# A two-layer encoder on one core: one more K pair per feed-forward block computed as seven products instead of eight, and silu as one activation function

## The chip, the core and the metric

The kernel runs on one core of one Trainium2 chip. A core has five engines that run side by side, each taking its own instructions in the order of the program: TensorE (PE in the profile; PEld is its loading of stationary operands), VectorE (DVE), ScalarE (ACT), GpSimd (POOL) and SyncE (SP, which here issues the DMAs). They wait for each other by semaphores. The metric is device time in microseconds (us) for one execution.

## The reference

The input is 256 tokens of 2048 float32. Layer 0 mixes tokens by differential attention and a gated spatial mixer, layer 1 by a bidirectional gated recurrence; each is followed by a feed-forward network. The change touches the feed-forward network (and one buffer count in layer 1's mixer):

```python
def swiglu(h, w_gate, w_up, w_down):
    return (jax.nn.silu(h @ w_gate) * (h @ w_up)) @ w_down

hn = rms_norm(h, ffn_norm[l])          # in both layers l = 0, 1
h = h + swiglu(hn, ffn_w_gate[l], ffn_w_up[l], ffn_w_down[l])
```

`w_gate` and `w_up` are 2048 x 5632, `w_down` is 5632 x 2048.

## The kernel before

Every matrix product is done in float32 accuracy from float32r operands: a weight tile `raw` arrives by DMA, ScalarE rounds it to `whi` (L310), VectorE computes the rest `wlo = raw - whi` (L320), and TensorE does three matmuls per product, `x_hi*w_hi`, `x_hi*w_lo`, `x_lo*w_hi` (L297 to L299).

**The feed-forward network.** The 5632 hidden columns are 11 blocks `j` of 512. They come in groups (0, 1), (2, 3, 4), (5, 6, 7), (8, 9, 10): for each block of a group `gate_up` computes gate and up for both halves (`b` = 0, 1) of the tokens; after a group the product with `w_down` of its blocks is added to `h` (`stream`, with lighter work for VectorE). The K dimension of 2048 is eight pairs `p` of two 128-row chunks. One DMA of 1 MB brings the four 128x512 weight blocks of a pair: gate and up, each for both chunks. Gate and up for both token halves of a pair are a 2x2 by 2x2 block product. `PAIRS` says how a pair is done in blocks 1 to 10 (block 0 is plain):

- `N`: eight products (24 matmuls) into four accumulators.
- `S`: seven products (21 matmuls) of sums of blocks, as in the Strassen-Winograd scheme, into seven accumulators `P1` to `P7`, which fill seven PSUM banks `ps0` to `ps6`. The sums of token blocks (`combos`) are made once per layer during block 0. The sums of weight blocks are made per pair: three additions on VectorE into `t` (L316, L317, L318), a cast to `thi` on ScalarE (L319) and `tlo = t - thi` on VectorE (L322). `whi` and `wlo` of such a pair have three parts and not four.

`t`, `thi` and `tlo` have one buffer each, `wlo` two, `raw` and `whi` three. The bank of an accumulator is free for the next block when VectorE or ScalarE has read it.

**The end of a block** (L425 to L450). After the last `S` pair, `u1`, `u2`, `u3` are formed from `P1`, `P6`, `P7` (L430 to L432). After the last pair VectorE forms `gs[0]` from `P2` and `gs[1]` from `P4` (L444, L445), `hh[0]` and `hh[1]` from `P5` (L446, L447), and adds `P3` to `hh[0]` (L448); silu follows as a sigmoid on ScalarE (L406) and a product on VectorE (L407); then `hh = hh * r * gs` (L410). In the next block `hh` is transposed on TensorE (L206, tiles `tp0`, `tp1`) into the operand of the `w_down` product.

**What sets the order.** The instructions of each engine are put in order when the program is built, by a planner with priorities: `high_priority(offset=AHEAD)` lets the weight preparation of a pair go ahead of other work, the block's end has twice that offset. TensorE's order is planned too: the first matmul of a product may stand ahead of products whose `wlo` or `tlo` comes later. On the chip each engine keeps the planned order.

Of the kernel before, what the change touches and what calls it, by code (L numbers as in the profile page):

```python
# [11 lines left out]
F32 = mybir.dt.float32  # L12
# [4 lines left out]
ALU = mybir.AluOpType  # L17
# [3 lines left out]
P = 128  # L21
# [51 lines left out]
def trunk(ctx: ExitStack, tc: tile.TileContext, ins, out):  # L73
# [210 lines left out]


    P1, P2, P3, P4, P5, P6, P7 = range(7)
    PAIRS = "NSNSNSNN"

    def gate_up(l, j, xs, combos, fx, name, plain, after):
        pattern = "N" * 8 if plain else PAIRS  # L290
        bk = [bank("mm", [P, NB], f"{name}_ps{i}") for i in range(4 if plain else 7)]
        uses = {"S": [P1, P2, P3, P6, P7, P4, P5], "N": [0, 1, 2, 3] if plain else [P2, P4, P5, P3]}
        seen, final = set(), {b: p for p in range(8) for b in uses[pattern[p]]}

        def product(b, p, x, w, end):
# [6 lines left out]
        for p in range(8):  # L302
# [28 lines left out]
            def w(i):  # L331
                return whi[:, i], wlo[:, i]

            if plain:
                for b, c, i in ((0, 0, 0), (0, 1, 1), (1, 0, 0), (1, 1, 1), (2, 0, 3), (2, 1, 2), (3, 0, 3), (3, 1, 2)):
                    product(b, p, x(c, b % 2), w(i), c == 1)
                    if (b, c) == (1, 1):
                        tick()
            elif fast:
                def sums(i):  # L340
                    return combos[p][0][:, i], combos[p][1][:, i]

                def tw(i):
                    return thi[:, i], tlo[:, i]

                product(P1, p, x(0, 0), w(0), True)
                product(P2, p, x(1, 0), w(1), True)
                product(P3, p, sums(2), w(2), True)
                product(P6, p, sums(1), tw(2), True)
                product(P7, p, sums(3), tw(1), True)  # L350
                product(P4, p, x(1, 1), tw(3), True)
                product(P5, p, sums(0), tw(0), True)
            else:
                for c in range(2):
                    product(P2, p, x(c, 0), w(c), c == 1)
                for c in range(2):
                    product(P4, p, x(c, 1), w(c), c == 1)
                for c in range(2):
                    product(P5, p, x(c, 1), w(3 - c), c == 1)
                for c in range(2):  # L360
                    product(P3, p, (combos[p][0][:, c], combos[p][1][:, c]), w(3 - c), c == 1)
# [4 lines left out]
    def make_combos(xs, cp, combos, name):  # L366

        for p in range(8):
            xh, xl = xs.get(p)
            xt = _ap(xh, 0, [[KG * S, 2], [S, KG], [1, S]]).bitcast(F32)  # L370
            k0 = p % 2 * 2
            n = 4 if PAIRS[p] == "S" else 2
            c = [cp.tile([P, n, P], F32R, tag=f"c{p}{i}", name=f"{name}_c{p}{i}", bufs=1) for i in range(2)]
            parts = tmp.tile([P, 2, n, P], F32, tag="hh", name=f"{name}_cp{p}", bufs=2)

            def x(k, b):
                return xt[:, :, k0 + k, b * P:(b + 1) * P]

            if n == 4:

                nc.vector.tensor_tensor(parts[:, :, 0], x(0, 1), x(1, 1), op=ALU.subtract)
                nc.vector.tensor_tensor(parts[:, :, 1], parts[:, :, 0], x(0, 0), op=ALU.subtract)
                nc.vector.tensor_tensor(parts[:, :, 2], parts[:, :, 1], x(1, 0), op=ALU.add)
                nc.vector.tensor_tensor(parts[:, :, 3], x(0, 0), x(0, 1), op=ALU.subtract)
            else:
                for k in range(2):
                    nc.vector.tensor_tensor(parts[:, :, k], x(k, 0), x(k, 1), op=ALU.subtract)
            nc.vector.tensor_tensor(parts[:, 0], parts[:, 0], parts[:, 1], op=ALU.add)
            nc.scalar.copy(c[0], parts[:, 0])
            nc.vector.tensor_tensor(c[1], parts[:, 0], c[0].bitcast(F32), op=ALU.subtract)  # L390
            combos.append(c)
            yield

    def ffn(l, xs, rstd, following):

        with tc.tile_pool(name=f"hT{l}", bufs=3, reuse_waits="tile") as hp:
# [5 lines left out]
                return rstd()[:, b:b + 1]  # L402

            def silu(g, src, b, n):
                sg = fx.tile([P, NB], F32, tag="u", name=f"{n}_s{b}", bufs=3)
                nc.scalar.activation(sg, src, AF.Sigmoid, scale=r(b))  # L406
                nc.vector.scalar_tensor_tensor(out=g, in0=src, scalar=r(b), in1=sg, op0=ALU.mult, op1=ALU.mult)  # L407

            def gated(out, src, b, g):
                nc.vector.scalar_tensor_tensor(out=out, in0=src, scalar=r(b), in1=g, op0=ALU.mult, op1=ALU.mult)  # L410
# [1 line left out]
            for blocks in (range(0, 2), range(2, 5), range(5, 8), range(8, 11)):  # L412
                halves = Lazy()
                for j in blocks:
# [18 lines left out]
                                early["u"] = u1, u2, u3  # L433

                    bk = gate_up(l, j, xs, combos, fx, n, plain, after)
                    hh = tmp.tile([P, 2, NB], F32, tag="hh", name=f"{n}_hh", bufs=2)
                    with tc.high_priority(offset=2 * AHEAD):
                        if plain:
                            for b in range(2):
# [425 lines left out]

    for nb in range(4):
        ps = proj_c(16 + nb, f"g{nb}", after=at_end(early) if nb == 3 else None)
        gt = tmp.tile([P, 2, NB], F32, tag="hh", name=f"g{nb}t", bufs=2)
        gated(ps, gt, True)
        if nb == 3:  # L870
            finish_pieces()
        nc.vector.tensor_tensor(o[nb], gt, o[nb], op=ALU.mult)
        xo.makers.append(lambda nb=nb: to_T(o[nb], xpool, "xT", f"co{nb}", gain_cols(SM_GN, nb)))
# [138 lines left out]
```

## Time and profile before

| | |
|---|---|
| time, three runs | 2432.55 to 2434.47 us, median 2433.96 us |
| the profiled execution | 2432.7 us, its span 2430.9 us |
| TensorE busy | 2403.7 us (99%), 11212 matmuls, mean granted clock 0.998 |
| VectorE busy | 1747.8 us (72%) |
| ScalarE busy | 1136.2 us (47%) |
| DMA | 445.50 MB, the weights' queue 52.1% of the 16 engines' span |

The span is from the first instruction to the last; the 1.8 us beside it lie around the span. A matmul is shown with a modelled duration that overlaps the next one, so its pace is read from starts, not from durations. A wait is shown as idle time before an instruction with the one that ended it.

### The profile page before, as it was taken

How to read it: one execution, taken by the hardware profiler on the slowest of the kernel's cores; microseconds unless marked ns; L12 is line 12 of the kernel's file. 1: busy time of each engine (PE TensorE's matmuls, PEld its weight loads, DVE VectorE, ACT ScalarE, POOL GpSimd, SP SyncE). 2: the span in 40 equal slices, each digit the busy share in tenths (PEclk: the TensorE clock that was granted, in tenths of full speed). 3: DMA queues.
4: the chain of work that ended last, by engine and by line, in shares of the span. 5: the costliest groups of instructions: out<-in, count | busy, mean ns of one | idle time of the engine just before them, and what ended most of it. 6: DMA issues, size and time to landing. Idle time of an engine off the chain costs nothing.

```text
span 2430.9 us, 27555 instructions
## 1 busy us (share of the span) xinstructions
PE 2403.7 (99%) x11212; PEld 1993.8 (82%) x11212; DVE 1747.8 (72%) x1680; ACT 1136.2 (47%) x1048; POOL 72.9 (3%) x72
## 2 busy tenths in 40 slices
PE   8999999999999999999999999999999999999998
PEld 7887878888888888888888888888788888888887
DVE  5658667688678678754758595855777867876884
ACT  5445454445345445454444444444444544544553
POOL 0003000000000000000000000000000000000002
PEclk9999999999999999999999999999999999999999
DMA  7444455555555555555444444445455555565553
GB/s 275 169 160 168 160 180 184 190 194 204 191 202 196 191 198 190 201 198 191 156 145 151 156 139 156 144 168 190 169 195 200 187 201 191 190 208 190 208 208 139
DMA packets 63135, 445.50 MB, mean 183 GB/s; under 512 B 6944, under 2 KB 7200, under 8 KB 9760
## 3 DMA queue, kind: packets, MB, share of 16 engines
q1 hardware_dynamic: 62576, 442.13, 52.1%
q8 instruction: 88, 1.44, 0.2%
q10 hardware_dynamic: 432, 1.60, 0.2%
q14 instruction: 39, 0.32, 0.0%
HBM read 441.61 MB, written 2.10 MB: 183 GB/s over the span
## 4 chain that ended last, share of the span: by engine, by line
PE 94%; DVE 3%; POOL 1%; issue 1%; DMA 1%; ACT 0%; SPq 0%; ACTq 0%; POOLq 0%; DVEq 0%
PE f_ps L298 12%; PE f_ps L297 12%; PE f_ps L299 12%; PE f0d_ps L164 3%; PE f0d_ps L166 3%; PE f0d_ps L165 3%; PE f1d_ps L164 3%; PE f1d_ps L165 3%; PE f1d_ps L166 3%; PE c_f_ps L166 2%; PE c_f_ps L164 2%; PE c_f_ps L165 2%; PE s_l L759 2%; PE c_q_ps L166 1%; PE c_q_ps L164 1%; PE c_q_ps L165 1%
## 5 line engine op out<-in xcount | busy, mean ns | idle before, releaser
L310 ACT CAST f_whi<-f_raw 128x2048 fp32r<-128x2048 f32 (+1 forms) x176 | 311.2, 1768 | 248.7 <-PE f_ps L299 162.5
L320 DVE TENSOR_TENSOR f_wlo<-f_raw,f_whi 128x2048 fp32r<-128x2048 f32 (+1 forms) x176 | 368.7, 2106 | 47.0 <-PE f_ps L298 33.2
L297 PE MATMUL f_ps<-f_whi,f_x 128*128 128x512 f32 x848 | 331.3, 393 | 6.1 <-DVE h L883 3.1
L299 PE MATMUL f_ps<-f_whi,f_x 128*128 128x512 f32 x848 | 330.3, 390 | 0.0
L298 PE MATMUL f_ps<-f_wlo,f_x 128*128 128x512 f32 x848 | 330.1, 389 | 0.0
L297 PEld LDWEIGHTS f_ps<-f_whi,f_x 128*128 128x128 f32 x848 | 159.2, 188 | 38.8 <-ACT f_j L182 6.9
L299 PEld LDWEIGHTS f_ps<-f_whi,f_x 128*128 128x128 f32 x848 | 159.2, 188 | 33.6
L298 PEld LDWEIGHTS f_ps<-f_wlo,f_x 128*128 128x128 f32 x848 | 159.3, 188 | 32.2
L322 DVE TENSOR_TENSOR f_tlo<-f_t,f_thi 128x2048 fp32r<-128x2048 f32 x60 | 137.3, 2288 | 62.7 <-ACT f_thi L319 62.7
L319 ACT CAST f_thi<-f_t 128x2048 fp32r<-128x2048 f32 x60 | 114.8, 1913 | 132.3 <-DVE f_t L318 120.0
L149 ACT CAST f1d__whi<-f1d__raw 128x2048 fp32r<-128x2048 f32 x44 | 84.4, 1919 | 128.4 <-PE f1d_ps L166 97.6
L150 DVE TENSOR_TENSOR f1d__wlo<-f1d__raw,f1d__whi 128x2048 fp32r<-128x2048 f32 x44 | 100.8, 2290 | 60.6 <-PE f1d_ps L165 33.0
L150 DVE TENSOR_TENSOR f0d__wlo<-f0d__raw,f0d__whi 128x2048 fp32r<-128x2048 f32 x44 | 100.7, 2289 | 59.0 <-PE f0d_ps L165 29.3
L149 ACT CAST f0d__whi<-f0d__raw 128x2048 fp32r<-128x2048 f32 x44 | 84.4, 1918 | 122.1 <-PE f0d_ps L166 91.3
L150 DVE TENSOR_TENSOR c_f_wlo<-c_f_raw,c_f_whi 128x2048 fp32r<-128x2048 f32 x32 | 73.3, 2292 | 72.5 <-PE c_f_ps L165 60.5
L164 PE MATMUL c_f_ps<-c_f_whi,c_x 128*128 128x512 f32 x256 | 102.5, 400 | 0.0
L299 PE MATMUL f_ps<-f_whi,x_c 128*128 128x512 f32 x260 | 101.1, 389 | 0.0
L298 PE MATMUL f_ps<-f_wlo,x_c 128*128 128x512 f32 x260 | 101.1, 389 | 0.0
L297 PE MATMUL f_ps<-f_whi,x_c 128*128 128x512 f32 x260 | 101.1, 389 | 0.0
L166 PE MATMUL c_f_ps<-c_f_whi,c_x 128*128 128x512 f32 x256 | 100.2, 392 | 0.0
L165 PE MATMUL c_f_ps<-c_f_wlo,c_x 128*128 128x512 f32 x256 | 99.6, 389 | 0.0
L149 ACT CAST c_f_whi<-c_f_raw 128x2048 fp32r<-128x2048 f32 x32 | 61.2, 1913 | 77.6 <-PE c_f_ps L166 57.6
(536 smaller groups left out, 5637.1 us busy)
## 6 DMA issues: line engine op xcount, KB each, us to landing
f_raw<-in_w_gu SPq DMA_DIRECT2D x176, 1024.0 KB, 4.9
f0d__raw<-in_w_down SPq DMA_DIRECT2D x44, 1024.0 KB, 4.9
f1d__raw<-in_w_down SPq DMA_DIRECT2D x44, 1024.0 KB, 4.9
c_f_raw<-in_hgrn_w_in SPq DMA_DIRECT2D x32, 1024.0 KB, 4.9
eout_raw<-in_even_w_out SPq DMA_DIRECT2D x16, 1024.0 KB, 4.8
c_i_raw<-in_hgrn_w_in SPq DMA_DIRECT2D x16, 1024.0 KB, 4.8
c_q_raw<-in_hgrn_w_in SPq DMA_DIRECT2D x16, 1024.0 KB, 4.8
c_g_raw<-in_hgrn_w_in SPq DMA_DIRECT2D x16, 1024.0 KB, 4.9
```

What stands on the lines that cost most here:

```text
L149: nc.scalar.copy(whi[:, d], raw[:, d])
L150: nc.vector.tensor_tensor(wlo[:, d], raw[:, d], whi[:, d].bitcast(F32), op=ALU.subtract)
L164: nc.tensor.matmul(ps[b], xh[:, k, sl], hi[:, k, :], start=first, stop=False)
L165: nc.tensor.matmul(ps[b], xh[:, k, sl], lo[:, k, :], start=False, stop=False)
L166: nc.tensor.matmul(ps[b], xl[:, k, sl], hi[:, k, :], start=False, stop=end)
L297: nc.tensor.matmul(bk[b], xh, hi, start=b not in seen, stop=False)
L298: nc.tensor.matmul(bk[b], xh, lo, start=False, stop=False)
L299: nc.tensor.matmul(bk[b], xl, hi, start=False, stop=end and final[b] == p)
L310: nc.scalar.copy(whi[:, d], raw[:, d])
L319: nc.scalar.copy(thi, t)
L320: nc.vector.tensor_tensor(wlo[:, d], raw[:, d], whi[:, d].bitcast(F32), op=ALU.subtract)
L322: nc.vector.tensor_tensor(tlo, t, thi.bitcast(F32), op=ALU.subtract)
```

## The change

Four things change. (1) `PAIRS` goes from `NSNSNSNN` to `SNSNSNSN`: four of eight pairs are `S`, from the first pair of a block on, and the last pair is `N`. `combos` follow. (2) In an `S` pair the product `P3` is issued fifth and not third. (3) silu is one activation function on ScalarE, in place; the sigmoid's tile and the VectorE product (L407) go. (4) Tiles with the tag `hh` (a block's `hh`, the parts of `combos`, and `gt` in layer 1's mixer) have one buffer and not two.

```diff
--- before.py
+++ after.py
@@ -284,12 +284,12 @@
 
 
     P1, P2, P3, P4, P5, P6, P7 = range(7)
-    PAIRS = "NSNSNSNN"
+    PAIRS = "SNSNSNSN"
 
     def gate_up(l, j, xs, combos, fx, name, plain, after):
         pattern = "N" * 8 if plain else PAIRS
         bk = [bank("mm", [P, NB], f"{name}_ps{i}") for i in range(4 if plain else 7)]
-        uses = {"S": [P1, P2, P3, P6, P7, P4, P5], "N": [0, 1, 2, 3] if plain else [P2, P4, P5, P3]}
+        uses = {"S": [P1, P2, P6, P7, P3, P4, P5], "N": [0, 1, 2, 3] if plain else [P2, P4, P5, P3]}
         seen, final = set(), {b: p for p in range(8) for b in uses[pattern[p]]}
 
         def product(b, p, x, w, end):
@@ -345,9 +345,9 @@
 
                 product(P1, p, x(0, 0), w(0), True)
                 product(P2, p, x(1, 0), w(1), True)
-                product(P3, p, sums(2), w(2), True)
                 product(P6, p, sums(1), tw(2), True)
                 product(P7, p, sums(3), tw(1), True)
+                product(P3, p, sums(2), w(2), True)
                 product(P4, p, x(1, 1), tw(3), True)
                 product(P5, p, sums(0), tw(0), True)
             else:
@@ -371,7 +371,7 @@
             k0 = p % 2 * 2
             n = 4 if PAIRS[p] == "S" else 2
             c = [cp.tile([P, n, P], F32R, tag=f"c{p}{i}", name=f"{name}_c{p}{i}", bufs=1) for i in range(2)]
-            parts = tmp.tile([P, 2, n, P], F32, tag="hh", name=f"{name}_cp{p}", bufs=2)
+            parts = tmp.tile([P, 2, n, P], F32, tag="hh", name=f"{name}_cp{p}", bufs=1)
 
             def x(k, b):
                 return xt[:, :, k0 + k, b * P:(b + 1) * P]
@@ -402,9 +402,7 @@
                 return rstd()[:, b:b + 1]
 
             def silu(g, src, b, n):
-                sg = fx.tile([P, NB], F32, tag="u", name=f"{n}_s{b}", bufs=3)
-                nc.scalar.activation(sg, src, AF.Sigmoid, scale=r(b))
-                nc.vector.scalar_tensor_tensor(out=g, in0=src, scalar=r(b), in1=sg, op0=ALU.mult, op1=ALU.mult)
+                nc.scalar.activation(g, src, AF.Silu, scale=r(b))
 
             def gated(out, src, b, g):
                 nc.vector.scalar_tensor_tensor(out=out, in0=src, scalar=r(b), in1=g, op0=ALU.mult, op1=ALU.mult)
@@ -433,7 +431,7 @@
                                 early["u"] = u1, u2, u3
 
                     bk = gate_up(l, j, xs, combos, fx, n, plain, after)
-                    hh = tmp.tile([P, 2, NB], F32, tag="hh", name=f"{n}_hh", bufs=2)
+                    hh = tmp.tile([P, 2, NB], F32, tag="hh", name=f"{n}_hh", bufs=1)
                     with tc.high_priority(offset=2 * AHEAD):
                         if plain:
                             for b in range(2):
@@ -865,7 +863,7 @@
 
     for nb in range(4):
         ps = proj_c(16 + nb, f"g{nb}", after=at_end(early) if nb == 3 else None)
-        gt = tmp.tile([P, 2, NB], F32, tag="hh", name=f"g{nb}t", bufs=2)
+        gt = tmp.tile([P, 2, NB], F32, tag="hh", name=f"g{nb}t", bufs=1)
         gated(ps, gt, True)
         if nb == 3:
             finish_pieces()
```

The planner puts the work in another order. Two places show it, both where block 4 of layer 0 follows block 3 within a group. `f0_4_` names a tile of layer 0, block 4; the digit after `wlo`, `whi`, `t`, `thi`, `tlo` is the pair; `ps0` to `ps6` are `P1` to `P7`; what stands in brackets is whom the instruction waits for.

TensorE before, at the seam of pair 0 (`N`, whose 24 matmuls open the block) and pair 1 (`S`), the first pair with a tile that VectorE makes after the end of block 3:

```order
L299 MATMUL f0_4_ps2_4299<-f0_4_whi0_4305,x0_c01_2813 128x512
L297 MATMUL f0_4_ps0_4297<-f0_4_whi1_4335,f00_x_2612 128x512 [waits DVE_49,Activation_49]
L297 MATMUL f0_4_ps1_4298<-f0_4_whi1_4335,f00_x_2612 128x512
L298 MATMUL f0_4_ps0_4297<-f0_4_wlo1_4336,f00_x_2612 128x512 [waits DVE_49]
L299 MATMUL f0_4_ps0_4297<-f0_4_whi1_4335,f00_x_2612 128x512
L298 MATMUL f0_4_ps1_4298<-f0_4_wlo1_4336,f00_x_2612 128x512
L299 MATMUL f0_4_ps1_4298<-f0_4_whi1_4335,f00_x_2612 128x512
```

TensorE now, from the eighth matmul of the block on (seven on pairs 0 and 1, on `whi0`, `wlo0` and `whi1`, stand ahead of it):

```order
L297 MATMUL f0_4_ps0_4298<-f0_4_whi2_4379,f01_x_2665 128x512 [waits Activation_49]
L206 MATMUL f0_3T_tp0_4371<-ident_89,f0_3_hh_4286 128x128 [waits DVE_49,PE_49]
L206 MATMUL f0_3T_tp0_4371<-ident_89,f0_3_hh_4286 128x128 x3
L298 MATMUL f0_4_ps1_4299<-f0_4_wlo1_4342,f00_x_2612 128x512 [waits DVE_49]
L299 MATMUL f0_4_ps1_4299<-f0_4_whi1_4341,f00_x_2612 128x512
L297 MATMUL f0_4_ps1_4299<-f0_4_whi1_4341,f00_x_2612 128x512
L298 MATMUL f0_4_ps1_4299<-f0_4_wlo1_4342,f00_x_2612 128x512
L299 MATMUL f0_4_ps1_4299<-f0_4_whi1_4341,f00_x_2612 128x512
L297 MATMUL f0_4_ps1_4299<-f0_4_whi2_4379,f01_x_2665 128x512
L206 MATMUL f0_3T_tp1_4443<-ident_89,f0_3_hh_4286 128x128 [waits DVE_49]
L206 MATMUL f0_3T_tp1_4443<-ident_89,f0_3_hh_4286 128x128 x3
L297 MATMUL f0_4_ps5_4303<-f0_4_thi0_4311,x0_c00_2812 128x512 [waits Activation_49]
```

The first matmul on `wlo1` stood behind 26 matmuls of block 4 and the transposes of block 3's `hh` behind 37; both stand behind 8 now, and the products of pair 0 on `thi0` behind them.

VectorE before, from the addition of `P3` of block 3 on:

```order
L448 TENSOR_TENSOR f0_3_hh_4281<-f0_3_ps2_4000,f0_3_hh_4281 128x512 [waits DVE_49,PE_49]
L407 SCALAR_TENSOR_TENSOR f0_3_g1_3997<-f0_3_g1_3997,f0_rstd_3003,f0_3_s1_4290 128x512 [waits Activation_49]
L410 SCALAR_TENSOR_TENSOR f0_3_hh_4281<-f0_3_hh_4281,f0_rstd_3003,f0_3_g0_3996 128x512 [waits DVE_49]
L410 SCALAR_TENSOR_TENSOR f0_3_hh_4281<-f0_3_hh_4281,f0_rstd_3003,f0_3_g1_3997 128x512 [waits DVE_49]
L318 TENSOR_TENSOR f0_4_t1_4339<-f0_4_t1_4339,f0_4_raw1_4334 128x512
L320 TENSOR_TENSOR f0_4_wlo1_4336<-f0_4_raw1_4334,f0_4_whi1_4335 128x1536
L320 TENSOR_TENSOR f0_4_wlo2_4379<-f0_4_raw2_4377,f0_4_whi2_4378 128x2048 [waits DMAHW6_49,PE_49,Activation_49]
L322 TENSOR_TENSOR f0_4_tlo1_4341<-f0_4_t1_4339,f0_4_thi1_4340 128x2048 [waits Activation_49]
L320 TENSOR_TENSOR f0_4_wlo3_4409<-f0_4_raw3_4407,f0_4_whi3_4408 128x1536 [waits DVE_49,DMAHW7_49,PE_49,Activation_49]
```

VectorE now, from the same addition on:

```order
L446 TENSOR_TENSOR f0_3_hh_4286<-f0_3_ps2_4000,f0_3_hh_4286 128x512 [waits DVE_49,PE_49]
L408 SCALAR_TENSOR_TENSOR f0_3_hh_4286<-f0_3_hh_4286,f0_rstd_3005,f0_3_g1_3997 128x512 [waits DVE_49,Activation_49]
L408 SCALAR_TENSOR_TENSOR f0_3_hh_4286<-f0_3_hh_4286,f0_rstd_3005,f0_3_g0_3996 128x512 [waits DVE_49]
L317 TENSOR_TENSOR f0_4_t0_4310<-f0_4_t0_4310,f0_4_raw0_4305 128x512
L320 TENSOR_TENSOR f0_4_wlo1_4342<-f0_4_raw1_4340,f0_4_whi1_4341 128x2048 [waits DMAHW5_49]
L318 TENSOR_TENSOR f0_4_t0_4310<-f0_4_t0_4310,f0_4_raw0_4305 128x512 [waits DVE_49]
L210 TENSOR_TENSOR f0_3T_x_4370<-f0_3T_tp0_4371,f0_3T_x_4370 128x512 [waits Activation_49]
L322 TENSOR_TENSOR f0_4_tlo0_4312<-f0_4_t0_4310,f0_4_thi0_4311 128x2048 [waits Activation_49]
L320 TENSOR_TENSOR f0_4_wlo2_4380<-f0_4_raw2_4378,f0_4_whi2_4379 128x1536 [waits DMAHW6_49,PE_49]
```

One instruction of silu is gone from between; the end of block 3 still stands ahead of the sums and the `wlo` of block 4's `S` pair, which is now pair 0 and not pair 1; `wlo1` is now the full tile of an `N` pair.

## Rows read from the trace of the kernel before

**Rows 1.** The page's busy times: engine, us, share of the span, instructions.
```profile
PE 2403.7 (99%) x11212; PEld 1993.8 (82%) x11212; DVE 1747.8 (72%) x1680; ACT 1136.2 (47%) x1048; POOL 72.9 (3%) x72
```

**Rows 2.** The page's chain that ended last, by engine.
```profile
PE 94%; DVE 3%; POOL 1%; issue 1%; DMA 1%; ACT 0%; SPq 0%; ACTq 0%; POOLq 0%; DVEq 0%
```

**Rows 3.** Windows of blocks 2, 3, 4 of layer 0, columns as named.
```profile
core 0: us, PE busy (x) PEld busy (x) DVE busy (x) ACT busy (x) POOL busy (x), PEclk, DMA share, GB/s
494.32:535.80 41.48, 41.48 (x184) 34.35 (x183) 33.59 (x26) 20.67 (x13) 0.00 (x0) 1.00 0.56 202
535.80:578.25 42.45, 42.45 (x193) 35.13 (x192) 36.57 (x34) 21.14 (x16) 0.00 (x0) 1.00 0.56 197
578.25:621.16 42.91, 42.91 (x193) 34.95 (x191) 37.19 (x33) 23.15 (x17) 0.00 (x0) 1.00 0.57 199
```

**Rows 4.** Timeline of PE, first matmuls of blocks 2 and 3: start, us.
```profile
494.32 0.39 PE L297 MATMUL f_ps<-f_whi,f_x 128*128 128x512 f32 x1
...
535.80 0.39 PE L297 MATMUL f_ps<-f_whi,f_x 128*128 128x512 f32 x1
```

**Rows 5.** Timeline of DVE, the end of block 3 and after: start, us.
```profile
578.98 0.68 DVE L448 TENSOR_TENSOR f_hh<-f_ps,f_hh 128x512 f32<-128x512 f32 x1
579.58 0.74 DVE L407 SCALAR_TENSOR_TENSOR f_g<-f_g,f_rstd,f_s 128x512 f32<-128x512 f32 x1
580.24 1.41 DVE L410 SCALAR_TENSOR_TENSOR f_hh<-f_hh,f_rstd,f_g 128x512 f32<-128x512 f32 x2
581.56 0.69 DVE L318 TENSOR_TENSOR f_t<-f_t,f_raw 128x512 f32<-128x512 f32 x1
582.16 1.76 DVE L320 TENSOR_TENSOR f_wlo<-f_raw,f_whi 128x1536 fp32r<-128x1536 f32 x1
...
588.24 1.76 DVE L320 TENSOR_TENSOR f_wlo<-f_raw,f_whi 128x1536 fp32r<-128x1536 f32 x1
589.90 1.22 DVE L316 TENSOR_TENSOR f_t<-f_raw 128x1024 f32<-128x1024 f32 x1
591.04 0.69 DVE L210 TENSOR_TENSOR f_3T_x<-f_3T_tp,f_3T_x 128x512 fp32r<-128x512 f32 x1
...
594.49 2.29 DVE L320 TENSOR_TENSOR f_wlo<-f_raw,f_whi 128x2048 fp32r<-128x2048 f32 x1 [1.44 <-PE f_ps L298]
596.70 2.29 DVE L322 TENSOR_TENSOR f_tlo<-f_t,f_thi 128x2048 fp32r<-128x2048 f32 x1
```

**Rows 6.** Timeline of PE, a matmul that completes a bank.
```profile
648.40 0.39 PE L166 MATMUL f0d_ps<-f0d__whi,f_4T_x 128*128 128x512 f32 x1
```

**Rows 7.** Timeline of DVE, the instruction that waited for it.
```profile
648.83 0.69 DVE L279 TENSOR_TENSOR h<-f0d_ps,h 128x512 f32<-128x512 f32 x1 [2.63 <-PE f0d_ps L166]
```

**Rows 8.** Timeline of DVE, a tlo that TensorE waited for.
```profile
789.69 2.28 DVE L322 TENSOR_TENSOR f_tlo<-f_t,f_thi 128x2048 fp32r<-128x2048 f32 x1
```

**Rows 9.** Timeline of PE, the matmul that waited for it.
```profile
792.03 0.50 PE L298 MATMUL f_ps<-f_tlo,x_c 128*128 128x512 f32 x1
```

**Rows 10.** Chain in order of time, eight transposes: start, us.
```profile
340.84 0.87 PE f_tp L206 x8
```

**Rows 11.** Groups of ACT and DVE instructions: count, busy us, mean ns, idle before.
```profile
L319 ACT CAST f_thi<-f_t 128x2048 fp32r<-128x2048 f32 x60 | 114.8, 1913 | 132.3 <-DVE f_t L318 120.0 <-PE f_ps L298 5.8 <-PE f_ps L299 5.0
L406 ACT ACTIVATE f_s<-f_g,f_rstd 128x512 f32<-128x512 f32 x40 | 28.9, 722 | 28.6 <-DVE f_g L444 15.4 <-DVE f_g L407 13.2
L406 ACT ACT_TABLE_LOAD x1 | 1.3, 1283 | 0.0
L407 DVE SCALAR_TENSOR_TENSOR f_g<-f_g,f_rstd,f_s 128x512 f32<-128x512 f32 x40 | 29.8, 747 | 1.5 <-ACT f_s L406 1.3
```

**Rows 12.** Timeline of PE, a wait as layer 0's feed-forward network begins.
```profile
362.84 0.47 PE L297 MATMUL f_ps<-f_whi,f_x 128*128 128x512 f32 x1 [3.00 <-DVE h L279]
```

**Rows 13.** Window around that wait, columns as in Rows 3.
```profile
360.00:365.00 5.00, 2.16 (x10) 1.83 (x11) 4.76 (x9) 4.10 (x7) 0.35 (x1) 1.00 0.37 110
```

## The prediction

> **What bounds the kernel now.** I read the page's busy times first: TensorE is busy 99% of the span, VectorE 72% [rows 1]. The chain that ended last says the same from the other side: 94% of it runs over TensorE and 3% over VectorE [rows 2]. So the time is the number of matmuls times their pace, as long as TensorE isn't kept waiting. The third view is windows over the stage that the change touches, three blocks of one group: 41.48, 42.45 and 42.91 us [rows 3]. Block 2 has 3 x 21 + 5 x 24 = 183 matmuls and nothing else on TensorE, and its first matmul stands 41.48 us ahead of block 3's [rows 4]: 41.48 / 183 = 0.2267 us a matmul. Blocks 3 and 4 hold eight transposes besides, 0.87 us [rows 10]; what is left over, 0.10 and 0.56 us, is waiting. The reader is to see two things in those windows: TensorE has no slack there, and VectorE rises from 33.6 to 36.6 to 37.2 us of about 42 [rows 3]. It is the second tightest engine, just where the change gives it more.
>
> **What goes.** One more S pair in each of the 10 fast blocks of two layers: 20 x 3 = 60 matmuls, 60 x 0.2267 = 13.6 us, all on the path, since TensorE is it. That is the whole gain. The product of silu on VectorE also goes, 40 x 0.747 us [rows 11], but off the path, except where the end of a block is.
>
> **What is added off the path.** An S pair costs VectorE three sums (1.22, 0.69, 0.69) and a tlo (2.29), less 0.53 for the smaller wlo (2.29 to 1.76) [rows 5]: 4.4 us a block, against 1.5 saved on silu. Block 4 would come to about 37.2 + 2.9 = 40.1 us. Its work on TensorE is 180 matmuls and eight transposes, 40.8 + 0.9 = 41.7 us, so VectorE still fits, with 4% to spare: as a sum it does not become the bound, but there is nothing left to make good a delay in the same block. ScalarE gets one thi more a block, 1.91 us [rows 11], and is busy 23 of 43 us [rows 3]. Silu stands where the sigmoid stood; I take its 0.72 us [rows 11]. Its table must be loaded in each layer, with the mixer's sigmoid table between: two more loads of 1.283 us [rows 11], on an engine that idles 20 us a block, taken as nothing (2.6 us if all of it showed). The single `hh` buffer costs nothing: a block's `hh` is read by transposes early in the next block and written again at that block's end.
>
> **What moves: the seam between blocks.** Before, a block began with an N pair, and its 24 matmuls, 5.4 us, covered the end of the block ahead. Now it begins with the S pair. Let T be the start of the new block's first matmul, and take block 3 to block 4 as the order gives it.
>
> VectorE's side. Its steps follow each other at 0.60 us for a 512-column addition (578.98 to 579.58), 0.66 for a product with two scalars, 1.14 for the first sum, 1.66 for a wlo of an S pair, 2.21 for a full wlo or a tlo [rows 5]. The last wlo of block 3 (pair 7) waits until TensorE has read the buffer for the last time in pair 5, 47 matmuls ahead of T: -10.65 us, and 0.43 from a matmul's start until a waiting VectorE starts (648.40 to 648.83) [rows 6, 7], so it starts at -10.2. From there VectorE has no gap: wlo, tlo of pair 6, wlo of the new pair 0, u2, gs[0], u3, first sum, gs[1], two hh: 2.21 + 2.21 + 1.66 + 3 x 0.60 + 1.14 + 3 x 0.60 = 10.8. The addition of P3, which needs the very last matmul (ready at +0.20), starts at +0.6. Then 0.60, the two products with gs (0.66 each, the last one lasting 0.75): hh is done at +2.6. A sum (0.60), and wlo1 from +3.1 to +5.4. The last sum ends at +6.0, and thi0 on ScalarE, 1.91 us, at +8.0.
>
> TensorE's side. Eight matmuls bring it to +1.8. It wants hh for four transposes and gets it at +2.7 (a wlo or tlo reaches a waiting matmul 0.06 us after its end, 791.97 to 792.03 [rows 8, 9]): 0.9 us of waiting. At +3.1 it wants wlo1, and gets it at +5.5: 2.4 us. Six matmuls and four transposes later, at +7.3, it wants thi0 and gets it at +8.0: 0.7 us. Then 11 matmuls end at +10.5, when tlo0 (8.0 + 2.3) is there. In all 3.9 us, in program order, with matmuls that could run standing behind. Behind wlo1 on VectorE stand the sum that thi0 needs and tlo0, so its delay is passed on.
>
> The first seam of a group (block 2 to 3) is different: coming from the light w_down stage, VectorE has made t0, thi0 and tlo0 before the end of block 2, and the same reckoning gives no wait. The order has the late form in blocks 4, 7 and 10 of both layers, word for word alike: six seams. Within a block the order puts first matmuls ahead of a late tlo, and the reckoning has each tlo there 0.0 to 0.3 us in time; I allow 0.05 us for each of the 48 S pairs of the later blocks of groups, 2.4 us.
>
> **The sum,** against the profiled execution's own 2432.7 us (span 2430.9): -13.6 for matmuls; +6 x 3.9 = +23.4 at the seams; -6 x 0.56 = -3.4, since the waiting that such a block has now is part of what is laid out anew; +2.4. That makes +8.8: 2441.5. The median of the runs is 1.3 above the profiled one, so 2443 us, slower by 0.4%.
>
> The seam is the term that the trace does not show, so both ends: below, VectorE not behind at T (0.4 less) and thi0 hidden (0.7 less), 2.8 us a seam, and the sum is 2436; above, tlo late by 0.3 us in each of those 48 pairs as well, 14.4 in place of 2.4, 2455. I take the reckoned 3.9, since every duration in it has a row and the order fixes who waits for whom.
>
> **Rivals.**
> - *Gain without the wait* (faster): TensorE finds something else to do, and 13.6 us come off whole: 2420. For: the blocks wait only 0.10 and 0.56 us now [rows 3], so the planner has hidden such things so far. Against: it hid them behind the N pair, and the order shows eight matmuls there. Chance 0.10.
> - *Short seam* (no change): the chain on VectorE is 0.4 us early and thi0 comes in time, no small waits: 6 x 2.8 - 3.4 - 13.6 = -0.2, 2434. Chance 0.14.
> - *VectorE becomes the bound all along a group*: 40.1 of 41.7 us leaves no room for its own waits, and each tlo of the 48 pairs comes 0.5 us late. The place is the tlo that TensorE waits for, and it decides from the point where VectorE's sum and waits pass 41.7 us: 2443 - 2.4 + 24 = 2465. For: in block 4 it idles 5.7 us, partly waiting for TensorE and thi [rows 3, 11]. Against: those waits shrink when it is late. Chance 0.09.
> - *The clock falls at the seams.* Rows: TensorE waited 3.00 us once, and the granted clock of that window was 1.00, the 2.4 GHz level [rows 12, 13]; the new waits are 2.4 us at most. If the clock halved after each seam for an S pair's 21 matmuls, 6 x 21 x 0.2267 = 28.6 us would be added: 2472. Chance 0.02. The Trainium skill, "TensorE: Matmul & The Clock Gate", section "HAM oscillation — how this bites in real kernels", speaks for this one: waits between groups of matmuls can put the clock back again and again. By that rule the time would be the 2472; the row of the 3.00 us wait doesn't bear it out.
>
> **How the numbers follow.** The forecast has 0.65. A difference under 0.2%, 4.9 us, can't be told from no change here, so slower is above 2438.8 and faster below 2429.1. Of the forecast's 0.65 about 0.04 lies under 2438.8 (a seam near its low end). Slower: 0.61 + 0.09 + 0.02 = 0.72; same: 0.14 + 0.04 = 0.18; faster: 0.10. The forecast's own range is 2436 to 2455. The range for 8 in 10 takes in the short seam and reaches a little towards the late tlo: 2432 to 2458.
>
> **What would show it.** Right: TensorE at 60 matmuls fewer; blocks 2, 5 and 8 at 40.8 us; block 3 near 41.7; blocks 4, 7 and 10 at 45 to 46, with waits ahead of a transpose, the first matmul on wlo1 and the first on thi0, put down to VectorE and ScalarE; VectorE without a gap from the last wlo to the new wlo1. Wrong: block 4 at 42 (no wait), waits spread over every tlo (VectorE bound), or a granted clock under 1.00 after the seams. A silu much longer than 0.72 us, or a weight tile that lands late, would change the terms that I set at nothing.

## The result, and the profile after

The changed kernel takes 2454.32 us (median of four runs, 2452.95 to 2454.68) against 2434.22 us of the kernel before beside it: ratio 1.0077 [1.0062, 1.0092], slower by 20 us. The forecast was 2443 (2432 to 2458): slower was right, but by 9 us where 20 came. The profiled execution took 2454.7 us, its span 2452.9 us, 22.0 more than before. Its busy times and its chain, which answer to [rows 1, 2]:

```profile
PE 2410.1 (98%) x11152; PEld 1988.6 (81%) x11152; DVE 1803.8 (74%) x1720; ACT 1168.6 (48%) x1070; POOL 72.3 (3%) x72
```

```profile
PE 92%; DVE 5%; issue 1%; POOL 1%; DMA 0%; ACT 0%; SPq 0%; ACTq 0%; POOLq 0%; DVEq 0%
```

60 matmuls are gone, VectorE has 56 us more, and its share of the chain rose from 3% to 5%. The same windows as in [rows 3], blocks 2, 3, 4 of layer 0, and then blocks 5, 6, 7:

```profile
core 0: us, PE busy (x) PEld busy (x) DVE busy (x) ACT busy (x) POOL busy (x), PEclk, DMA share, GB/s
494.21:535.01 40.80, 40.80 (x181) 33.78 (x180) 34.04 (x27) 22.97 (x15) 0.00 (x0) 1.00 0.55 193
535.01:577.38 42.37, 42.37 (x189) 34.41 (x188) 39.23 (x35) 21.97 (x16) 0.00 (x0) 1.00 0.53 191
577.38:624.49 47.11, 44.71 (x190) 35.50 (x188) 40.90 (x35) 24.53 (x18) 0.00 (x0) 0.96 0.57 197
690.77:731.57 40.80, 40.80 (x182) 33.78 (x180) 34.04 (x27) 22.98 (x15) 0.00 (x0) 1.00 0.56 194
731.57:773.91 42.34, 42.34 (x190) 34.41 (x188) 39.22 (x35) 21.95 (x16) 0.00 (x0) 1.00 0.52 191
773.91:820.18 46.27, 43.34 (x189) 34.24 (x188) 40.91 (x35) 24.42 (x18) 0.00 (x0) 1.00 0.57 201
```

The first block of a group is 0.7 us shorter, the middle one about as long as before, the third some 4 us longer. VectorE is busy 40.9 us in the third, whose TensorE work is 41.7 us. Block 4's clock is 0.96, block 7's 1.00.

TensorE at the clean seam, block 6 to 7, whose first matmul starts at T = 773.91:

```profile
775.27 0.92 PE L297 MATMUL f_ps<-f_whi,f_x 128*128 128x512 f32 x2
776.49 0.63 PE L206 MATMUL f_6T_tp<-ident,f_hh 128*128 128x128 f32 x4 [0.30 <-DVE f_hh L408]
779.21 0.50 PE L298 MATMUL f_ps<-f_wlo,f_x 128*128 128x512 f32 x1 [2.08 <-DVE f_wlo L320]
779.54 0.40 PE L299 MATMUL f_ps<-f_whi,f_x 128*128 128x512 f32 x1
...
780.70 0.60 PE L206 MATMUL f_6T_tp<-ident,f_hh 128*128 128x128 f32 x4
781.80 0.73 PE L297 MATMUL f_ps<-f_thi,x_c 128*128 128x512 f32 x2 [0.51 <-ACT f_thi L319]
782.38 0.39 PE L297 MATMUL f_ps<-f_whi,x_c 128*128 128x512 f32 x1
...
784.43 0.39 PE L298 MATMUL f_ps<-f_tlo,x_c 128*128 128x512 f32 x1
```

From start to start, less the 0.2267 us of a matmul (0.44 of four transposes), the stalls are 0.77 before the transposes, 2.28 before wlo1, 0.66 before thi0, and 0.10 and 0.13 right behind the last two: 3.94 us. VectorE over the same seam, which answers to [rows 5]:

```profile
763.54 2.29 DVE L320 TENSOR_TENSOR f_wlo<-f_raw,f_whi 128x2048 fp32r<-128x2048 f32 x1 [1.65 <-PE f_ps L298]
...
774.34 0.69 DVE L446 TENSOR_TENSOR f_hh<-f_ps,f_hh 128x512 f32<-128x512 f32 x1
774.93 1.41 DVE L408 SCALAR_TENSOR_TENSOR f_hh<-f_hh,f_rstd,f_g 128x512 f32<-128x512 f32 x2
...
776.86 2.29 DVE L320 TENSOR_TENSOR f_wlo<-f_raw,f_whi 128x2048 fp32r<-128x2048 f32 x1
779.06 0.69 DVE L318 TENSOR_TENSOR f_t<-f_t,f_raw 128x512 f32<-128x512 f32 x1
...
781.78 2.29 DVE L322 TENSOR_TENSOR f_tlo<-f_t,f_thi 128x2048 fp32r<-128x2048 f32 x1 [1.43 <-ACT f_thi L319]
```

VectorE works without a gap from T - 10.4 to T + 6.4. ScalarE makes thi0 from T + 5.93 to T + 7.84:

```profile
779.84 1.91 ACT L319 CAST f_thi<-f_t 128x2048 fp32r<-128x2048 f32 x1 [2.10 <-DVE f_t L318]
```

The granted clock, in windows of 4 us over the seam of block 4 and that of block 7, and then over the start of layer 1's feed-forward network, columns as above:

```profile
580.00:584.00 4.00, 1.92 (x9) 1.40 (x10) 3.81 (x4) 1.29 (x2) 0.00 (x0) 0.93 0.20 29
584.00:588.00 4.00, 4.00 (x15) 3.28 (x14) 2.77 (x2) 2.18 (x3) 0.00 (x0) 0.65 0.89 371
776.00:780.00 4.00, 1.61 (x8) 1.09 (x8) 4.00 (x5) 0.74 (x2) 0.00 (x0) 1.00 0.00 0
780.00:784.00 4.00, 3.50 (x18) 2.70 (x17) 2.57 (x3) 2.23 (x2) 0.00 (x0) 1.00 0.90 342
```

```profile
1720.00:1724.00 4.00, 2.92 (x7) 2.37 (x8) 3.54 (x10) 1.61 (x5) 0.69 (x1) 0.51 0.63 221
```

At the seam of block 4 the granted clock drops to the 1.2 GHz level for some 3 us, at that of block 7, with the same waits for hh and wlo1, it does not. It fell at four of the six seams; the matmuls ahead of thi0 then run slower, and no wait for thi0 is left there. It fell once more as layer 1's feed-forward network starts, in a wait of 3.46 us; there the kernel before waited 3.12 us and kept its clock.

### The profile page after: what moved, and what is told of

Same layout as the page of the kernel before. It is cut to its first block, busy times and chain, and to the rows that moved or that the text cites. A ratio compares the mean times of both kernels' runs of the same rounds, so it can differ in the third digit from the quotient of the medians.

```text
span 2452.9 us, 27534 instructions
## 1 busy us (share of the span) xinstructions
PE 2410.1 (98%) x11152; PEld 1988.6 (81%) x11152; DVE 1803.8 (74%) x1720; ACT 1168.6 (48%) x1070; POOL 72.3 (3%) x72
## 4 chain that ended last, share of the span: by engine, by line
PE 92%; DVE 5%; issue 1%; POOL 1%; DMA 0%; ACT 0%; SPq 0%; ACTq 0%; POOLq 0%; DVEq 0%
PE f_ps L298 12%; PE f_ps L297 12%; PE f_ps L299 12%; PE f0d_ps L165 3%; PE f0d_ps L164 3%; PE f0d_ps L166 3%; PE f1d_ps L166 3%; PE f1d_ps L164 3%; PE f1d_ps L165 3%; PE c_f_ps L166 2%; PE c_f_ps L164 2%; PE c_f_ps L165 2%; PE s_l L757 2%; PE c_q_ps L166 1%; PE c_q_ps L164 1%
## 5 line engine op out<-in xcount | busy, mean ns | idle before, releaser
L310 ACT CAST f_whi<-f_raw 128x2048 fp32r<-128x2048 f32 (+1 forms) x176 | 302.5, 1719 | 251.0 <-PE f_ps L299 144.8
L298 PE MATMUL f_ps<-f_wlo,f_x 128*128 128x512 f32 x768 | 302.1, 393 | 12.5 <-DVE f_wlo L320 12.5
L297 PE MATMUL f_ps<-f_whi,f_x 128*128 128x512 f32 x768 | 302.3, 396 | 7.0 <-DVE h L881 3.5
L299 PE MATMUL f_ps<-f_whi,f_x 128*128 128x512 f32 x768 | 301.2, 392 | 0.0
L319 ACT CAST f_thi<-f_t 128x2048 fp32r<-128x2048 f32 x80 | 152.9, 1912 | 157.5 <-DVE f_t L318 152.9
L322 DVE TENSOR_TENSOR f_tlo<-f_t,f_thi 128x2048 fp32r<-128x2048 f32 x80 | 183.0, 2288 | 56.3 <-ACT f_thi L319 56.3
L298 PEld LDWEIGHTS f_ps<-f_wlo,f_x 128*128 128x128 f32 x768 | 145.2, 189 | 44.8 <-DVE f_wlo L320 15.3
L297 PEld LDWEIGHTS f_ps<-f_whi,f_x 128*128 128x128 f32 x768 | 145.5, 189 | 40.1 <-ACT f_j L182 7.6
L299 PEld LDWEIGHTS f_ps<-f_whi,f_x 128*128 128x128 f32 x768 | 145.2, 189 | 30.4
L316 DVE TENSOR_TENSOR f_t<-f_raw 128x1024 f32<-128x1024 f32 x80 | 97.7, 1221 | 1.0 <-DMA f_raw<-in_w_gu 0.2
L298 PE MATMUL f_ps<-f_tlo,x_c 128*128 128x512 f32 x240 | 97.1, 405 | 0.0
L297 PE MATMUL f_ps<-f_whi,x_c 128*128 128x512 f32 x240 | 94.3, 393 | 0.0
```

Source lines behind the costliest of these rows:

```text
L297: nc.tensor.matmul(bk[b], xh, hi, start=b not in seen, stop=False)
L298: nc.tensor.matmul(bk[b], xh, lo, start=False, stop=False)
L299: nc.tensor.matmul(bk[b], xl, hi, start=False, stop=end and final[b] == p)
L310: nc.scalar.copy(whi[:, d], raw[:, d])
L319: nc.scalar.copy(thi, t)
L322: nc.vector.tensor_tensor(tlo, t, thi.bitcast(F32), op=ALU.subtract)
```

## The experiments

My theory after the trace: the seam is the loss, since the N pair that covered a block's end is gone; some 7 us come on top from the clock. Ratios are against the kernel before; 1.0077 is the changed kernel's.

**Silu alone.** In the kernel before:

```diff
-                sg = fx.tile([P, NB], F32, tag="u", name=f"{n}_s{b}", bufs=3)
-                nc.scalar.activation(sg, src, AF.Sigmoid, scale=r(b))
-                nc.vector.scalar_tensor_tensor(out=g, in0=src, scalar=r(b), in1=sg, op0=ALU.mult, op1=ALU.mult)
+                nc.scalar.activation(g, src, AF.Silu, scale=r(b))
```

> The kernel before with the third part of the change alone: silu as one ScalarE function (pairs NSNSNSNN, P3 third, two hh buffers). Theory (the loss lies at the seam between blocks, made by the new order of pairs): no change, 2431 to 2437 us; the end of a block loses a 0.60 us step on VectorE, two table loads of 1.28 us are added on ScalarE, and TensorE waits nowhere anew. Rival (silu as one function costs the time, by its tables or by a longer instruction): 10 to 20 us of the loss show here, 2444 or more.

2433.52 us, 0.9991 [0.9982, 1.0]. No loss lies here. Groups of three blocks take 126.36 us where the kernel before took 126.75 to 127.66. One thing more is in its trace: the wait of [rows 12], again 3.00 us. There the granted clock of the window was 1.00; here it falls:

```profile
363.63 0.76 PE L297 MATMUL f_ps<-f_whi,f_x 128*128 128x512 f32 x1 [3.00 <-DVE h L279]
```

```profile
364.00:368.00 4.00, 4.00 (x13) 3.10 (x13) 3.74 (x11) 1.17 (x4) 0.71 (x1) 0.65 0.73 258
```

**Three S pairs, S first.**

```diff
-    PAIRS = "SNSNSNSN"
+    PAIRS = "SNSNSNNN"
```

> The changed kernel with three S pairs and not four, an S pair still first: SNSNSNNN. The matmuls are as many as before. Theory (a seam waits because VectorE comes to the block's end late, from the S pair one place ahead of the last, AND no N pair covers it): two N pairs at the end let VectorE make the new block's sums early, so TensorE waits at most 1 us at a seam: 2432 to 2440 us, granted clock 1.00 at the seams. Rival (an S pair at the front of a block costs 3.9 us at six seams whatever the end is): 2434 + 23 = 2457 us, with waits ahead of a transpose, wlo1 and thi0.

2434.19 us, 0.9997 [0.9988, 1.0006]. The third and fourth part of the change and P3 fifth are in it, and an S pair opens each block: none of this costs time while VectorE has only three S pairs.

**Four S pairs, N first**, in two orders, the one of the diff and `NSNSNSNS`:

```diff
-    PAIRS = "SNSNSNSN"
+    PAIRS = "NSNS" "SNSN"
```

> The changed kernel with four S pairs in an order that begins with an N pair: NSNSSNSN. As many matmuls and as much VectorE work as in the changed kernel. Theory (the seam is the loss, not VectorE's sum): the N pair at the front covers the block's end again; the 13.6 us of fewer matmuls come through less small waits for late tlo tiles, two S pairs side by side among them: 2420 to 2432 us. Rival (with four S pairs VectorE, at 40.1 of 41.7 us, is the bound wherever they stand): 2445 to 2460 us, waits spread over the tlo tiles.

> The changed kernel with four S pairs alternating from the second on: NSNSNSNS, so no two S pairs are neighbours within a block and an N pair opens each block, but a block ends with an S pair. NSNSSNSN cost 2460 us, with waits before the first matmuls on thi of the second of two neighbouring S pairs. Theory (those waits came from the neighbours, which share the one buffer of t, thi and tlo): 2425 to 2440 us. Rival (VectorE has too little time with four S pairs wherever they stand): 2450 us or more, waits of 3 to 6 us in each group at other places.

2460.54 us, 1.0108 [1.0093, 1.0124], and 2452.52 us, 1.0073 [1.0058, 1.0088]. My theory fell twice: with an N pair in front the loss is as large. In the first, TensorE waits in the second and third block of a group; the two longest of its waits in blocks 2 to 4:

```profile
564.18 0.74 PE L297 MATMUL f_ps<-f_thi,x_c 128*128 128x512 f32 x2 [0.89 <-ACT f_thi L319]
...
608.51 0.72 PE L297 MATMUL f_ps<-f_thi,x_c 128*128 128x512 f32 x2 [1.12 <-ACT f_thi L319]
```

In the second, block 10 waits at its seam, as in the changed kernel and for the same tiles, and the clock fell behind it (0.63 in 980 to 984):

```profile
976.46 0.63 PE L206 MATMUL f_9T_tp<-ident,f_hh 128*128 128x128 f32 x4 [0.65 <-DVE f_hh L408]
978.63 0.50 PE L298 MATMUL f_ps<-f_wlo,f_x 128*128 128x512 f32 x1 [1.55 <-DVE f_wlo L320]
```

**Half of tlo left out.** VectorE computes two of the four parts of tlo, and these two serve for the other two as well, so the result is less exact.

```diff
-                    nc.vector.tensor_tensor(tlo, t, thi.bitcast(F32), op=ALU.subtract)
+                    nc.vector.tensor_tensor(tlo[:, 0:2], t[:, 0:2], thi[:, 0:2].bitcast(F32), op=ALU.subtract)
-                    return thi[:, i], tlo[:, i]
+                    return thi[:, i], tlo[:, i % 2]
```

> The changed kernel with half of VectorE's tlo left out: tlo = t - thi is computed for two of its four parts, and these two serve in place of the others, so the result is less exact. Every matmul stays, the order of pairs stays SNSNSNSN. VectorE has some 1.1 us less for each S pair, 4.4 us a block, about what the fourth S pair gave it. Theory (the waits come from VectorE arriving late at the end of a block; an S pair in front only shows it): the seam waits fall under 1 us, the late tlo tiles come in time, and the 60 matmuls fewer come through: 2434 - 13.6 = 2420, so 2418 to 2425 us. Rival (an S pair in front has no cover for the end of the block, whatever VectorE's load): over 2440 us.

2423.07 us, 0.9949 [0.9932, 0.9965]. The pairs and the number of matmuls are those of the changed kernel, and 31 us are gone. Blocks 5 to 7 as one window, where the changed kernel has 129.41 us, 114.17 of them VectorE's:

```profile
687.64:812.48 124.84, 124.84 (x558) 102.77 (x556) 103.43 (x95) 69.15 (x48) 0.00 (x0) 1.00 0.59 203
```

124.14 would be no wait at all (540 x 0.2267 + 1.74). So it is VectorE's load, and not what opens a block. But the planner, with less work for VectorE, also made another order. At the seam of blocks 6 and 7 (first matmul of block 7 at 770.46) thi0 and tlo0 are used from the seventh matmul on, and the transposes of hh stand behind 45 matmuls of block 7, where the changed kernel has 8:

```profile
771.82 0.39 PE L297 MATMUL f_ps<-f_thi,x_c 128*128 128x512 f32 x1
772.04 0.39 PE L298 MATMUL f_ps<-f_tlo,x_c 128*128 128x512 f32 x1
...
780.66 0.60 PE L206 MATMUL f_6T_tp<-ident,f_hh 128*128 128x128 f32 x4
```

In the run with three S pairs, S first, the order at this seam is the same. So the run shows what VectorE's load does together with the order that the planner makes for it, and does not tell the two apart.

**TensorE kept busy in the waits.** `fill` is a part of the layer's input, for the `hh` of blocks 3, 6 and 9 only (the lines that hand it over are left out here):

```diff
             tp = bank("tr", [P, 2, S], f"{name}_tp{h}")
+            if fill is not None and h == 0:
+                for _ in range(14):
+                    nc.tensor.matmul(tp, fill[:, 0, :P], fill[:, 0:2], start=True, stop=True)
```

> The changed kernel with 14 matmuls that compute nothing that is used, 3.17 us at full clock, into the transposes' own bank ahead of the first transposes at the six seams with a wait; they need only the layer's input, so TensorE works where it waited. Nothing is waited for earlier: VectorE and ScalarE set when hh, wlo1 and thi0 are there. Theory (of the 20 us lost some 4 to 5 come from the clock that fell to 1.2 GHz behind four of the six seams, the rest from the waits): the granted clock stays 1.00 at all six seams, their summed idle time is under 1 us each, and the time falls by 3 to 6 us: 2448 to 2451. Rival (the lower clock costs nothing, since TensorE would only have waited longer for VectorE): no change, 2453 to 2456. Second rival (14 matmuls more delay what follows): slower, up to 6 x 3.2 = 19 us, 2473.

2451.0 us, 1.0065 [1.0052, 1.0077]: 3.3 us below the changed kernel, though TensorE does 19 us more work. The intervals of the two ratios overlap; the groups below show the gain more plainly. The fill at the seam of block 7, and what came next:

```profile
776.74 3.34 PE L205 MATMUL f_6T_tp<-f_x 128*128 128x512 f32 x14
779.92 0.60 PE L209 MATMUL f_6T_tp<-ident,f_hh 128*128 128x128 f32 x4
780.27 0.48 PE L300 MATMUL f_ps<-f_whi,f_x 128*128 128x512 f32 x1
```

The granted clock stayed 1.00 at all six seams, and all six groups took 129.29 to 129.44 us. In the changed kernel they took 129.40 and 129.41 where the clock held and 130.21, 130.26, 130.28 and 131.35 where it fell. The lower clock cost 0.81 + 0.86 + 0.88 + 1.95 = 4.5 us at the seams.

**P3 third again** (the same move in `uses` is left out here):

```diff
                 product(P2, p, x(1, 0), w(1), True)
+                product(P3, p, sums(2), w(2), True)
                 product(P6, p, sums(1), tw(2), True)
                 product(P7, p, sums(3), tw(1), True)
-                product(P3, p, sums(2), w(2), True)
```

> The changed kernel with P3 issued third again in an S pair (the second part of the change undone). Theory (the sum of the waits at a seam is set by when VectorE and ScalarE have hh, wlo1, thi0 and tlo0; P3's three matmuls, 0.68 us, only move from behind thi0 to ahead of hh): same time as the changed kernel, 2450 to 2457 us; the first wait shrinks, one at tlo0 takes its place. Rival (P3 fifth makes the seam longer, or shorter): off by 6 x 0.7 = 4 us or more, 2448 or 2459.

2445.1 us, 1.0042 [1.0027, 1.0057]: 9 us better than the changed kernel; the rival holds. The seam of block 7, T = 774.83:

```profile
777.55 0.60 PE L206 MATMUL f_6T_tp<-ident,f_hh 128*128 128x128 f32 x4
780.13 0.50 PE L298 MATMUL f_ps<-f_wlo,f_x 128*128 128x512 f32 x1 [1.98 <-DVE f_wlo L320]
...
782.98 0.62 PE L297 MATMUL f_ps<-f_thi,x_c 128*128 128x512 f32 x2
...
785.39 0.48 PE L298 MATMUL f_ps<-f_tlo,x_c 128*128 128x512 f32 x1
```

```profile
780.77 1.92 ACT L319 CAST f_thi<-f_t 128x2048 fp32r<-128x2048 f32 x1 [1.99 <-DVE f_t L318]
```

The dates that VectorE and ScalarE set are the same as in the changed kernel: the first matmul on wlo1 starts at T + 5.30 in both, and thi0 is done at T + 7.86 here and at T + 7.84 there. But with P3 third the planner puts 12 matmuls ahead of the first of these dates and 12 between the two, with P3 fifth 8 and 6 (and four transposes more). TensorE waits neither for hh nor for thi0 now. The first matmul on tlo0, for which it waits in neither kernel, starts at T + 10.56 here and at T + 10.52 there. By then 34 matmuls and six transposes are done here, 34 x 0.2267 + 0.65 = 8.36 us, and 25 and eight there, 6.54 us. The idle time is what is left: 2.2 and 4.0 us. I had taken P3's own three matmuls alone. Groups took 128.09 to 128.20, and at no seam did the clock fall.

**Part of wlo on GpSimd.**

```diff
-                nc.vector.tensor_tensor(wlo[:, d], raw[:, d], whi[:, d].bitcast(F32), op=ALU.subtract)
+                dv = d if plain else slice(0, 3)
+                nc.vector.tensor_tensor(wlo[:, dv], raw[:, dv], whi[:, dv].bitcast(F32), op=ALU.subtract)
+                if not plain and not fast:
+                    nc.gpsimd.tensor_tensor(wlo[:, 3], raw[:, 3], whi[:, 3].bitcast(F32), op=ALU.subtract)
```

> The changed kernel with the last of the four parts of each N pair's wlo (128x512) made on GpSimd and not on VectorE; nothing is left out. VectorE has 0.55 us less for each N pair, 2.2 us a block. GpSimd took 2.28 us for such a subtraction or product elsewhere in the kernel, and the part is wanted 12 matmuls, 2.7 us, behind the first of its pair. Theory (VectorE's lateness is the loss): the seam waits get shorter by 1.5 us or more and the small tlo waits go: 2428 to 2442 us. Rival (GpSimd's part comes late, or VectorE runs slower beside it): TensorE waits before a matmul on wlo in N pairs, no gain, 2450 us or more.

2463.26 us, 1.0118 [1.0102, 1.0133]. Worse, by the rival's second half. VectorE and GpSimd, each by its timeline, at one place:

```profile
745.16 1.76 DVE L321 TENSOR_TENSOR f_wlo<-f_raw,f_whi 128x1536 fp32r<-128x1536 f32 x1 [1.45 <-PE f_ps L298]
746.83 3.38 DVE L325 TENSOR_TENSOR f_tlo<-f_t,f_thi 128x2048 fp32r<-128x2048 f32 x1
```

```profile
745.18 2.89 POOL L323 TENSOR_TENSOR f_wlo<-f_raw,f_whi 128x512 fp32r<-128x512 f32 x1 [9.68 <-PE f_ps L298]
```

A tlo of 2.29 us took 3.38 with the GpSimd subtraction beside its first part; the wlo before it, beside the same subtraction, kept its 1.76. Over the kernel the 160 wlo of three parts took 1.99 us on average (1.76 before) and the 80 tlo 2.54 (2.29): 57 us lost, against 43 saved by 80 x 0.535.

**A third wlo buffer**, in the kernel with P3 third (the lines that make room for it, by forming `gs[0]` in `u1`, are left out here):

```diff
-            wlo = wpool.tile([P, 4, NB], F32R, tag="wlo", name=f"{name}_wlo{p}", bufs=WLO_BUFS)
+            if pattern[p] == "S":
+                wlo = fx.tile([P, 3, NB], F32R, tag="wlos", name=f"{name}_wlo{p}")
+            else:
+                wlo = wpool.tile([P, 4, NB], F32R, tag="wlo", name=f"{name}_wlo{p}", bufs=WLO_BUFS)
```

> The changed kernel with P3 third (2445 us) and a third buffer for wlo within the feed-forward network (the S pairs get their own; the room comes from forming gs[0] in u1). Nothing is left out. At the seam VectorE's chain of 10 us started only when TensorE let go of a wlo buffer, after 1.63 us of idle time. Theory (that buffer sets when the chain can start): VectorE starts up to 1.6 us earlier, the wait of 2.1 us for wlo1 shrinks to about 0.5, six seams give back 8 to 10 us: 2434 to 2439 us. Rival (the planner spends the new freedom on preparing wlo of the next block ahead of tlo of the pair before, so that the tlo is late instead): waits of 1 us or more before matmuls on tlo, 2443 us or more.

2444.67 us, 1.0042 [1.0028, 1.0056]: nothing gained on the 2445.1 us of P3 third. TensorE waits elsewhere, in block 7 mostly before these:

```profile
781.16 0.50 PE L298 MATMUL f_ps<-f_wlo,f_x 128*128 128x512 f32 x1 [1.37 <-DVE f_wlo L323]
783.75 0.74 PE L297 MATMUL f_ps<-f_thi,x_c 128*128 128x512 f32 x2 [0.49 <-ACT f_thi L322]
806.35 0.50 PE L297 MATMUL f_ps<-f_whi,f_x 128*128 128x512 f32 x1 [0.96 <-ACT f_whi L313]
```

The time agrees with the rival, but the tile that it named was only a small part of it (a stall of 0.38 us for a tlo, at 769.72). The third buffer moved the waits and did not remove them; VectorE's busy time stayed as it was, 1806.7 us against 1802.5 with P3 third.

**Three S pairs in the middle block only** (the lines for the one more pair of token sums are left out here):

```diff
+    MIDDLE = "SNSNSNNN"
+    def pairs(j):
+        return MIDDLE if j in (3, 6, 9) else PAIRS
-        pattern = "N" * 8 if plain else PAIRS
+        pattern = "N" * 8 if plain else pairs(j)
```

> The changed kernel with three S pairs (SNSNSNNN) in the middle block of each group of three (blocks 3, 6, 9) and four in the others; nothing is left out, and one more pair of token sums is made per layer. 14 x 3 = 42 matmuls fewer than the kernel before, 9.5 us. Theory (VectorE reaches the seam late only after two blocks with four S pairs in a row; with three in the middle one it has made the sums and wlo of the third block ahead of its start): no wait of over 0.6 us at the six seams, groups of three at 543 x 0.2267 + 1.74 + 0.8 = 125.6 us, and 2434.5 - 9.5 + 2 = 2424 to 2430 us in all. Rival (VectorE is late at any seam with a block of four S pairs beside it): the groups keep 3 us of waits or more, 2436 us or more.

2426.63 us, 0.9965 [0.9952, 0.9977]: faster than both kernels, 8.5 us below the kernel before, where 42 matmuls fewer are worth 9.5 us; no part of the result is left out. Blocks 5 to 7, against 125.6 expected:

```profile
687.78:813.33 125.55, 125.55 (x560) 103.25 (x559) 109.71 (x91) 68.11 (x47) 0.00 (x0) 1.00 0.58 201
```

## Why the prediction came out as it did

**Right: the matmuls and the seam, by place and size.** 60 matmuls are gone and a block of four S pairs without a wait takes 40.80 us. All six seams wait for hh and wlo1 as laid out, the two that kept their clock for thi0 too. Reckoned from T: hh at +2.6, wlo1 at +5.4, thi0 at +8.0, 3.9 us of waiting; the clean seam shows +2.4, +5.2, +7.8 and 3.94. Silu's function takes 0.725 us. Two table loads more, the single `hh` buffer and ScalarE cost nothing that the run of silu alone or that of three S pairs could show.

**Wrong: the sum.** It gave 2441.5 for the profiled execution, 13.2 us too little. The measured 2454 lies inside the stated range, near its upper end, but this is partly luck: that end stood for tlo tiles 0.3 us late in 48 pairs, 12 us more, and what came is 5.6 us of small waits and 7.2 us of the clock, which has no place in the range. Three terms were mis-sized:

- *The small waits*, allowed at 2.4 us. A group with its clock took 129.41; 124.14 of it is work and 3.94 the seam, so 1.33 are small waits, 6 x 1.33 = 8.0 us, 5.6 more. A late tlo, five of them in blocks 5 to 7, costs a stall of about 0.05 and another 0.11 at the matmul behind it; I had 0.05 for both. One late wlo there cost 0.27, and I had no term for it.
- *The clock at the seams*, held at no cost, with a rival of chance 0.02 against it: 4.5 us. It fell at four seams, which the prediction had named as a sign of being wrong, and was low for 3 to 7 us; so the rival's place was right, its 28.6 us too much. I had ruled it out by one wait of 3.00 us with clock 1.00 [rows 12, 13], as if one wait that passed showed that none would fall. At that very place, in waits of 3.00 to 3.35 us, the clock fell in six of the twelve traces of this case; the kernel before was one of the others. The Trainium skill, "TensorE: Matmul & The Clock Gate", section "HAM oscillation — how this bites in real kernels", says that waits between groups of matmuls can put the clock back again and again; four seams of six bear it out.
- *The clock at the start of layer 1's feed-forward network*, for which there was no term: blocks 0 and 1 took 89.07 us where 87.01 - 0.68 = 86.33 was due, 2.7 us. It does not come from the new pairs: the run of silu alone, with three matmuls more, took 89.72 there. The clock fell here in the traces of all eleven kernels that have silu as one function, in two of them in a wait of 3.12 us, as long as that of the kernel before; it held in the one trace of the kernel before. Whether that part of the change brings the fall, or chance kept it away in that one trace, is not shown.

That leaves 13.2 - 5.6 - 4.5 - 2.7 = 0.4 us. The waits as these two networks start are 0.35 us longer each, and there are smaller differences, less 0.9 us by which one group of the kernel before, at 127.66, had been longer than the others.

**Half right: the cause.** I wrote that the N pair in front covered a block's end, and that VectorE, as a sum, was not the bound. With an N pair in front four S pairs cost as much, and with an S pair in front three cost nothing. What decides is VectorE's load: 39.2 and 40.9 us of work in two blocks running whose TensorE work is 41.7 us, and waits of its own for thi and for wlo buffers. With the full load the kernel took 2444.7 to 2460.5 us in each of the five orders that were run; three kernels with an S pair in front and less work on VectorE took 2423 to 2434, and in the one with half of tlo nothing else was changed. How the load acts is not shown in full: each run was planned anew, and none changed the load and kept the changed kernel's order, so the late tiles and the order with few matmuls ahead of them are not told apart. The rival of VectorE as the bound was nearer to why; it was wrong in where, since the waiting falls mostly on one seam and not on 48 tlo. Its point of decision, VectorE's sum with its waits, is the one to keep: with half of tlo 11.5 of the 13.6 us of the 60 matmuls came through, and with three S pairs in one block of three 8.5 of the 9.5 us of the 42 that remain.

**A part that I priced at nothing and that cost 9 us:** P3 fifth. I read the planned order at the seam, but not against an order with P3 third, which has nine more matmuls to run before tlo0. The spans of the two profiled executions differ by 9.4 us: the six groups are 1.3 us shorter each than those of the changed kernel at full clock, 7.8 us, and the 4.5 us of the lower clock at the seams are gone too; 1.6 us went back where the clock fell as layer 0's network starts, and 1.0 us ahead of it.

**Open:** why the clock fell at four seams and not at the two others with the same waits; and what VectorE's full load would cost in an order like that of the run with half of tlo.

## What to carry to other kernels

When a change trades the bound engine's work for work on the second tightest, compare the two engines stage by stage, with the second one's own waits counted in, and over two stages running: here a group with 110 us of VectorE's work to 124.8 of TensorE's waited 0.7 us, one with 114 to 124.1 waited 5.3, and spending the trade only where there was slack kept the gain. Where a stall is set by a date on another engine, count the work that the order puts ahead of that date: with the dates the same, it made the difference between 4.0 and 2.2 us of waiting. One wait that leaves the clock alone does not show that the next one will.

## What the runs showed of the hardware

- The granted clock fell to the 1.2 GHz level for some 3 to 7 us, in or right behind waits of some 2.4 to 4 us in all, but not at each: six like seams gave four falls, and the wait of 3.00 to 3.35 us as layer 0's network starts gave six falls in twelve traces. Runs of one kernel differ in it: the kernel before took 2431.9 us in an execution with mean clock 0.999 and 2436.9 in one with 0.997. Useless matmuls in the waits kept it at 1.00 at all six seams.
- A VectorE subtraction of 128x2048 float32 took 3.38 us instead of 2.29 when a GpSimd subtraction of 128x512 (2.89 us) ran beside its first part.
- A matmul that ends a wait is followed by about 0.1 us of further stall: 0.33 us from start to start (779.21 to 779.54) where the pace is 0.2267.
